# A hybrid encoder trunk on one core: unnormalised keys, with the squared norms put into the blocks' inversion, and six changes to the order of transfers and groups

## The chip, the core and the metric

The kernel runs on one core of a Trainium2 chip. The metric is the device time of one execution in microseconds, the median of three timed runs. A profile is of one further execution.

## The reference

The input is 1024 tokens of width 1024 in float32. Two layers follow, each a mixer and a SwiGLU feed-forward network (FFN, hidden width 2816) with RMS norms ahead of them, and a final norm. Layer 0 mixes with spatial gating and pooling, layer 1 with RWKV-7 time mixing, where the change lies:

```python
r = xr @ w_r; k = xk @ w_k; v = xv @ w_v
wlog = -jax.nn.softplus(-(w0 + jnp.tanh(xw @ w1) @ w2)) - 0.5
a = jax.nn.sigmoid(a0 + (xa @ a1) @ a2)
g = jax.nn.sigmoid(xg @ g1) @ g2
kk = heads(k * k_k)
kk = kk / jnp.maximum(jnp.sqrt(jnp.sum(kk * kk, axis=-1, keepdims=True)), 1e-12)
k = k * (1 + (a - 1) * k_a)
decay = heads(jnp.exp(-jnp.exp(wlog)))
# scan over the tokens, state S of 64x64 per head, inputs -kk and kk*a:
#   S = S*w + (S @ (-kk)) outer (kk*a) + v outer k ;  y = S @ r
y = wkv7_scan(rh, decay, kh, vh, -kk, kk * ah)
y = group_norm(y) * ln_w + ln_b
bonus = jnp.sum(rh * kh * r_k, axis=-1, keepdims=True) * vh
return ((y + bonus) * g) @ w_o
```

## The kernel before, in words

The tokens are two halves h of 512; a matrix product goes over blocks of 128 columns. Float32 products are made of three matmuls with operands split in a high and a low part (`mm3`, L399 to L401). Weights come in a fixed list (`plan`): ACT loads a block into `raw` (L121), ACT makes its high part (L157), DVE its low part (L158), and `take` hands the blocks out in list order. So the pushes in the list and the takes in the program must agree. Each engine runs its own instructions in a fixed order, which a scheduler has drawn from the program with priorities; the program can force an order of issue with `tc.issue_after`.

The stages that the change touches, in order of time:

- The FFN of layer 0 writes its hidden values to DRAM (`hid_d`). The down-projection of half 0 (`down_steps`, L883) goes over groups of two and three blocks (D0A): it loads the hidden blocks (`hd`, `ahi`, `alo`; L894), takes the weights and adds each sum to the residual H[0]. The residuals lie in DRAM too (`hm_d`); L1885 and L1891 load them. The same for half 1 (D0B[0]) runs beside the low-rank and gate products of half 0 (`beside`; LOWRANK_AT, GATE_AT and MIX_AT say after how many groups they come).
- `project(h)` makes, for eight pairs of heads p, the block of k, its square (for the norm), decays, r, and from them the scaled keys `ar` and `bk`. Ahead of that the gate's product is copied to `g_d` by ACT through buffers epx and k (L1212). For each pair, matmuls with a two-column indicator sum the squares (L1314) and the bonus (L1260). The norm is inverted on DVE and POOL (L1316, L404), sent to all rows by eight matmuls (L1333), and multiplied into the key (`kkn`, L1339). `interact` (L1238) multiplies keys and stores 32x32 blocks to `at_d`; after every fourth pair they are loaded as `iat` (L1253), and `invert` solves the triangular blocks in 31 steps of two DVE instructions (L1413, L1418), a few at a time between the other work. The inverses go to `xi_d` (L1422). Then the value product follows (L1384 on).
- `recur(h)` runs eight chunks of the recurrence, with FFN matmuls of the other half beside them. It loads `ar`, `bk`, `uv` and XT (the inverses, L1487 and L1490) for each chunk; the state is kept on chip between the halves in `state_d`.
- At the end FFN groups G1A[2] and G1A[3] of half 0, the output projection of half 1 between them, and the FFN of half 1. In `ffn` the kinds of step are g (gate), u (up), t (take a down weight) and d (down).

## Time and profile before

| | |
|---|---|
| three timed runs, median (lowest to highest) | 2438.87 us (2436.91 to 2441.32) |
| the profiled execution, its own time | 2432.77 us |
| its span in the trace | 2431.1 us |
| mean granted TensorE clock | 0.987 |
| bytes moved by DMA | 342.17 MB, 140 GB/s over the span |

In a row of a trace L399 is line 399 of the kernel; `out<-in` names what an instruction writes and reads; a time in brackets is the idle time of the engine before it and what ended that. PE is TensorE's matmul, PEld its weight load; DVE, ACT, POOL and SP are the vector, scalar, GpSimd and sync engines; a q behind a name is the engine's DMA-issuing side.

### The profile page before, as it was taken

To read this page: it belongs to the slowest core of one execution; us is meant where nothing else is said; L and a number is where in the kernel's file an instruction comes from. 1 tells how busy PE (TensorE), PEld (TensorE's weight loads), DVE (VectorE), ACT (ScalarE), POOL (GpSimd) and SP (SyncE) were. 2 spreads that over 40 slices of the span, in tenths; PEclk is the share of its full clock that TensorE was granted. 3 is DMA by queue.
4 is the path that set the end of the run, shared out by engine and by line. 5 is a ranking of instruction groups with operands and counts; after the bars stand their busy time and mean duration, and the time that the engine had idled before them with its cause. 6 is when DMAs were issued, how large, how long until landed. Compare 5 with 4: busy or idle time off the path is not lost. (4 is left out here: it accounts for less than half of the span.)

```text
span 2431.1 us, 38203 instructions
## 1 busy us (share of the span) xinstructions
PE 2347.3 (97%) x15567; PEld 1917.3 (79%) x15567; DVE 1475.1 (61%) x2328; ACT 937.1 (39%) x1403; POOL 214.8 (9%) x246
## 2 busy tenths in 40 slices
PE   8999999999899999999999999999999999999998
PEld 6888888888687878777777778777878788888887
DVE  6445765655567857856767947866664536444443
ACT  6233444444214753423335744433332224322223
POOL 0200000000000033201100123201100001000001
PEclk9999999999999999999999999999999999999999
DMA  5114443324665565775435465675544423433231
GB/s 179 52 52 147 152 152 96 121 96 165 226 233 172 171 163 133 207 202 167 143 117 168 150 169 142 190 232 159 146 121 132 123 77 97 144 98 96 86 105 52
DMA packets 406767, 342.17 MB, mean 141 GB/s; under 512 B 78080, under 2 KB 351616, under 8 KB 405824
## 3 DMA queue, kind: packets, MB, share of 16 engines
q10 hardware_dynamic: 266048, 195.33, 27.0%
q1 hardware_dynamic: 140544, 144.41, 19.1%
q8 instruction: 122, 2.00, 0.3%
q14 instruction: 53, 0.43, 0.1%
HBM read 263.07 MB, written 76.61 MB: 140 GB/s over the span
## 5 line engine op out<-in xcount | busy, mean ns | idle before, releaser
L399 PE MATMUL mm<-ahi,whi 128*128 128x512 f32 x1376 | 541.0, 394 | 7.0 <-ACT whi L157 3.0
L400 PE MATMUL mm<-alo,whi 128*128 128x512 f32 x1376 | 541.7, 394 | 2.6 <-DVE alo L158 2.5
L401 PE MATMUL mm<-ahi,wlo 128*128 128x512 f32 x1376 | 539.7, 392 | 1.6 <-DVE wlo L158 1.6
L157 ACT ACTIVATE whi<-raw 128x1024 fp32r<-128x1024 f32 (+1 forms) x280 | 282.1, 1014 | 572.2 <-PE mm L400 441.7
L158 DVE TENSOR_TENSOR wlo<-raw,whi 128x1024 fp32r<-128x1024 f32 (+1 forms) x280 | 328.5, 1177 | 249.8 <-ACT whi L157 231.5
L399 PEld LDWEIGHTS mm<-ahi,whi 128*128 128x128 f32 x1376 | 258.7, 188 | 66.2 <-ACT whi L157 4.7
L400 PEld LDWEIGHTS mm<-alo,whi 128*128 128x128 f32 x1376 | 258.8, 188 | 60.6 <-DVE alo L158 5.6
L401 PEld LDWEIGHTS mm<-ahi,wlo 128*128 128x128 f32 x1376 | 258.7, 188 | 57.9 <-DVE wlo L158 2.9
L493 DVE TENSOR_TENSOR h<-h,mm 128x512 f32<-128x512 f32 x276 | 185.8, 684 | 149.4 <-PE mm L401 148.4
L399 PE MATMUL mm<-hidhi,wdhi 128*128 128x512 f32 x304 | 118.4, 398 | 3.2 <-ACT hidhi L958 2.5
L400 PE MATMUL mm<-hidlo,wdhi 128*128 128x512 f32 x304 | 120.0, 395 | 0.0
L401 PE MATMUL mm<-hidhi,wdlo 128*128 128x512 f32 x304 | 119.7, 394 | 0.0
L730 PE MATMUL mm<-ahi,whi 128*128 128x512 f32 x296 | 115.6, 390 | 0.0
L731 PE MATMUL mm<-alo,whi 128*128 128x512 f32 x296 | 115.2, 389 | 0.0
L732 PE MATMUL mm<-ahi,wlo 128*128 128x512 f32 x296 | 113.6, 389 | 0.0
L955 DVE TENSOR_TENSOR sg<-sg,mm 128x512 f32<-128x512 f32 x52 | 35.7, 687 | 119.8 <-PE mm L401 119.6
L157 ACT ACTIVATE wdhi<-raw 128x1024 fp32r<-128x1024 f32 x42 | 43.3, 1056 | 160.2 <-PE mm L400 137.0
L399 PE MATMUL mm<-hd,dhi 128*128 128x512 f32 x192 | 75.9, 396 | 13.8 <-DMA hd<-hid_d 11.4
L400 PE MATMUL mm<-hd,dhi 128*128 128x512 f32 x192 | 75.8, 395 | 0.0
L401 PE MATMUL mm<-hd,dlo 128*128 128x512 f32 x192 | 74.9, 393 | 0.0
L399 PEld LDWEIGHTS mm<-hidhi,wdhi 128*128 128x128 f32 x304 | 57.7, 190 | 16.5 <-ACT hidhi L958 2.9
L400 PEld LDWEIGHTS mm<-hidlo,wdhi 128*128 128x128 f32 x304 | 57.9, 190 | 12.3 <-issue 0.5
(395 smaller groups left out, 4274.2 us busy)
## 6 DMA issues: line engine op xcount, KB each, us to landing
raw<-in_ffn_w_down_dram ACTq DMA_DIRECT2D x88, 512.0 KB
raw<-in_ffn_w_gate_dram ACTq DMA_DIRECT2D x74, 512.0 KB
raw<-in_ffn_w_up_dram ACTq DMA_DIRECT2D x74, 512.0 KB
hid_d<-hid SPq DMA_DIRECT2D x36, 512.0 KB
hd<-hid_d SPq DMA_DIRECT2D x26, 512.0 KB
raw<-in_ab_w_in_dram ACTq DMA_DIRECT2D x16, 512.0 KB
raw<-in_ab_w_out_dram ACTq DMA_DIRECT2D x16, 512.0 KB
raw<-in_rwkv_w_r_dram ACTq DMA_DIRECT2D x16, 512.0 KB
```

What stands on the lines that cost most here:

```text
L157: act.activation(hi, src, AF.Copy)
L158: (eng or dve).tensor_tensor(out=lo, in0=src, in1=hi.bitcast(F32), op=ALU.subtract)
L399: pe.matmul(o, whi, xhi, start=first, stop=False)
L400: pe.matmul(o, whi, xlo, start=False, stop=False)
L401: pe.matmul(o, wlo, xhi, start=False, stop=last)
L493: dve.tensor_tensor(out=H[h][:, m, :], in0=H[h][:, m, :], in1=o, op=ALU.add)
L730: pe.matmul(o, wh[:, k, :], x[0][:, k, :], start=st, stop=False, skip_group_check=True)
L731: pe.matmul(o, wh[:, k, :], x[1][:, k, :], start=False, stop=False, skip_group_check=True)
L732: pe.matmul(o, wl[:, k, :], x[0][:, k, :], start=False, stop=k == 3, skip_group_check=True)
L955: dve.tensor_tensor(out=s, in0=s, in1=o, op=ALU.mult)
```

## The change

The key is no longer divided by its norm. `kkn` is now k times k_k alone, on ACT. Where the block's factors are loaded for the inversion, the squared norms are loaded with them (`n2_d`, through DRAM): the block's factors are divided by the squared norms of their second index, and the inverse's diagonal starts with its reciprocal instead of with one. So the inverse holds the factor that the two key factors had, and the eight broadcast matmuls, the maximum on DVE and POOL's power are gone. The four norm matmuls and the four bonus matmuls follow one another; after every fourth pair `sums` copies the four pairs' sums, transposes them with one matmul and stores them.

Six other places: (1) the first hidden blocks of the down-projection are loaded ahead of the residual, whose second part (`rest_a`) follows in pieces; (2) the second half's down-projection has four hidden slots instead of three, loads a group ahead, and takes every third weight from the general ring; (3) the gate copies use eight buffers instead of four; (4) in `recur` the loads of norm weights, gate and values wait until the next key load has been issued, and the state passes through DRAM between the halves; (5) the last two groups of half 0 run in one call, with the output projection of half 1 and its norm called after the down step of the first; the gate step of the second group thereby comes ahead of that down step; (6) the low-rank product of the second half comes after six steps instead of eight.

```diff
-LOWRANK_AT, GATE_AT, MIX_AT = (2, 8), (3, 8), (1, 2)
+LOWRANK_AT, GATE_AT, MIX_AT = (2, 6), (3, 8), (1, 2)
...
-    push_ffn(1, 0, G1A[2], push_act(("y", 1), y_d[1]))
-    for e in push_o(1):
-        e()
-    push_ffn(1, 0, G1A[3])
+    y1, o1 = push_act(("y", 1), y_d[1]), push_o(1)
+    for i, e in enumerate(e for e in ffn_events(G1A[2] + G1A[3], True) if e[0] != "d"):
+        if e == ("u", G1A[3][0][0]):
+            for go in o1:
+                go()
+        push_ffn_event(1, 0, *e)
+        if e[0] in "gu":
+            next(y1, None)
...
-    def down_steps(h, groups, wslot, hslot, ahead=True, after=None, between=iter(()), at={}, first={}):
-
-        held = {}
+    def down_steps(h, groups, wslot, hslot, ahead=True, after=None, between=iter(()), at={}, first={}, loaded=None):
+
+        held, loaded = {}, [] if loaded is None else loaded
...
-                    sp.dma_start(held[f].bitcast(F32), hid_d[h][:, f])
+                    loaded.append(sp.dma_start(held[f].bitcast(F32), hid_d[h][:, f]).ins)
...
+                if ahead and gi + 1 < len(groups):
+                    load(groups[gi + 1])
                 if gi in at:
                     at[gi]()
-                if ahead and gi + 1 < len(groups):
-                    load(groups[gi + 1])
...
+                if f[-1] in then:
+                    then[f[-1]]()
...
-            t = tmp(("epx", "k")[m % 2], 2)
+            t = tmp(("k", "epx", "av", "sg")[m % 4], 2)
...
+                d2 = iat[:, 31, :]
                 for q in range(2):
                     sp.dma_start(
-                        iat[q * 64 : q * 64 + 64].rearrange("b s t -> b (s t)"),
-                        at_d[h][q, p - 3 : p + 1].rearrange("p r c s t -> (p r c) (s t)"),
+                        iat[q * 64 : q * 64 + 64, 0:31].rearrange("b s t -> b (s t)"),
+                        at_d[h][q, p - 3 : p + 1].rearrange("p r c s t -> (p r c) (s t)")[:, : 31 * 32],
                     )
+                    sp.dma_start(
+                        d2[q * 64 : q * 64 + 64], n2_d[h][q, p - 3 : p + 1].rearrange("p r c t -> (p r c) t")
+                    )
+                dve.tensor_scalar(out=d2, in0=d2, scalar1=1e-24, scalar2=None, op0=ALU.max)
+                dve.reciprocal(d2, d2)
+                dve.tensor_tensor(out=iat[:, 0:31], in0=iat[:, 0:31], in1=bc(d2.unsqueeze(1), [P, 31, 32]), op=ALU.mult)
...
+        def sums(p):
+
+            rn = tmp("rn", 1, [P, 64])[:, :32]
+            act.activation(rn, bo[:, 40 + 8 * p : 72 + 8 * p], AF.Copy)
+            ot = auxt()
+            pe.transpose(ot[:32, :P], rn, ident)
+            t = nt.tile([P, HT], F32, tag="nsq", bufs=2, name="n2")[:32, :P]
+            act.activation(t, ot[:32, :P], AF.Copy)
+            for q in range(2):
+                sp.dma_start(
+                    n2_d[h][q, p - 3 : p + 1].rearrange("p r (j c) t -> (p r j) c t", c=2),
+                    t.rearrange("m (c q t) -> m q c t", q=2, t=32)[:, q],
+                )
...
-            n2 = bo[:, 64 + 8 * p : 72 + 8 * p]
-            rn = tmp("rn", 2, [P, 4, 2, 8])[:, 0, 0, :]
-
-            def norms(j):
-                pe.matmul(n2[:, 2 * j : 2 * j + 2], sq[:, j * P : (j + 1) * P], ind2, start=True, stop=True)
-                if j == 3:
-                    dve.tensor_scalar(out=rn, in0=n2[:, 0:8], scalar1=1e-24, scalar2=None, op0=ALU.max)
-                    rsqrt(rn)
-
-            small = [lambda j=j: norms(j) for j in range(4)]
-            if prev is not None:
-                small += [lambda j=j, pv=prev: bonus(pv[0], pv[3], j) for j in range(4)]
+            n2 = bo[:, 64 + 8 * p : 72 + 8 * p].rearrange("t (r j) -> t r j", j=4)
+            o = o_r
             if p:
                 o = mmt()
-                dense2(o, *take(("r", h, p)), xr, between=small)
-            else:
-                o = o_r
-                for go in small:
-                    go()
+                dense2(o, *take(("r", h, p)), xr)
+            for j in range(4):
+                pe.matmul(n2[:, :, j], sq[:, j * P : (j + 1) * P], ind2, start=True, stop=True)
+            if prev is not None:
+                for j in range(4):
+                    bonus(prev[0], prev[3], j)
+            if p % 4 == 3:
+                sums(p)
             invert_on(INV)
-            rb = auxt()
-            for j in range(4):
-                for r in range(2):
-                    pe.matmul(
-                        rb[rows[r], j * P : (j + 1) * P], bc(rn[:, 2 * j + r : 2 * j + r + 1], [P, 64]), ident,
-                        start=True, stop=True,
-                    )
             ar, bk = tmp("ar", 2, [P, 8, 2, 64]), tmp("bk", 2, [P, 8, 2, 64])
             kkn = tmp("kkn", 2)
-            dve.scalar_tensor_tensor(out=kkn, in0=kt, scalar=col(C_KK + p), in1=rb, op0=ALU.mult, op1=ALU.mult)
+            act.activation(kkn, kt, AF.Copy, scale=col(C_KK + p))
...
-        pool.memset(xf[:, 0:2048:65], 1.0)
+        dve.tensor_copy(xf[:, 0:2048:65], iat[:, 31, :])
...
-    state_d = const.tile([P, 8, 64], F32, name="state_d")
-    pool.memset(state_d, 0.0)
+    state_d = dram.tile([P, 8, 64], F32, name="state_d")
...
-            sp.dma_start(bk, bk_d[h][c])
+            keys[0] = sp.dma_start(bk, bk_d[h][c])
...
+                if c == 7:
+                    sp.dma_start(state_d, Sn)
...
-                    with tc.issue_after(loaded[0].ins):
+                    with tc.issue_after(loaded[0].ins), tc.issue_after(keys[0].ins):
...
+        if h:
+            sp.dma_start(S[0], state_d)
...
-    wslot, hslot = slots_of(f, 4, 3)
+    wslot, hslot = slots_of(f, 4, 4)
     odd = {g: i % 2 for i, gs in enumerate(D0A) for g in gs}
-    prime_b, steps_b = down_steps(1, D0B[0], wslot, hslot, False, lambda m: sp.dma_start(h_d[1, 0][:, m, :], H[1][:, m, :]))
+    third = {g[2] for g in D0B[0]}
+    prime_b, steps_b = down_steps(1, D0B[0], lambda f: whl() if f in third else wslot(f), hslot, True, lambda m: sp.dma_start(h_d[1, 0][:, m, :], H[1][:, m, :]))
     acc, add = running_sums(0)
+    hid_loads = []
+
+    def rest_a():
+        for k in range(4, KT, 2):
+            with tc.issue_after(hid_loads[-1]):
+                sp.dma_start(H[0][:, k : k + 2, :], hm_d[0][:, k : k + 2, :])
+
     prime_a, steps_a = down_steps(
-        0, D0A, lambda f: (lw, wslot)[odd[f]](f), lambda f: (lh, hslot)[odd[f]](f), after=add, at={len(D0A) - 1: prime_b}, first=first,
+        0, D0A, lambda f: (lw, wslot)[odd[f]](f), lambda f: (lh, hslot)[odd[f]](f), after=add, at={0: rest_a, len(D0A) - 1: prime_b}, first=first, loaded=hid_loads,
...
-    for k in range(4, KT, 2):
-        a_loaded = sp.dma_start(H[0][:, k : k + 2, :], hm_d[0][:, k : k + 2, :])
...
-            with tc.issue_after(a_loaded.ins):
+            with tc.issue_after(hid_loads[-1]):
                 sp.dma_start(H[1][:, k : k + 2, :], hm_d[1][:, k : k + 2, :])
...
-    drive(ffn(1, 0, hnA, f, G1A[2], between=take_act(("y", 1)), early=True))
-    exhaust(out_proj(1, ys))
-    hnB = norm_split(1, C_FFN + 8, b)
-    drive(ffn(1, 0, hnA, f, G1A[3], last=True, early=True))
+    hnB = []
+
+    def out_b():
+        exhaust(out_proj(1, ys))
+        hnB.extend(norm_split(1, C_FFN + 8, b))
+
+    drive(ffn(1, 0, hnA, f, G1A[2] + G1A[3], last=True, between=take_act(("y", 1)), early=True, then={G1A[2][0][-1]: out_b}))
```

SyncE's issues at the start of the down-projection, before (`hm_d_75` and `hm_d_76` hold the residuals of halves 0 and 1, `hid_d_77` half 0's hidden values):

```order
L743 DMA hid_d_78<-hid 128x1024
L1885 DMA h<-hm_d_75 128x1024 x2
L1891 DMA h<-hm_d_76 128x1024 x4
L894 DMA hd<-hid_d_77 128x1024 x3
L894 DMA ahi<-hid_d_77 128x1024
L894 DMA alo<-hid_d_77 128x1024
L894 DMA hd<-hid_d_77 128x1024 x3
```

The first three hidden blocks stand behind six residual loads. The same place now (L898 is the hidden load, L1903 and L1916 the residual's):

```order
L747 DMA hid_d_78<-hid 128x1024
L898 DMA hd<-hid_d_77 128x1024 x3
L1903 DMA h<-hm_d_75 128x1024 x2
L898 DMA hd<-hid_d_77 128x1024
L898 DMA ahi<-hid_d_77 128x1024
L898 DMA alo<-hid_d_77 128x1024
L1916 DMA h<-hm_d_76 128x1024 x2
L898 DMA hd<-hid_d_77 128x1024 x2
L1916 DMA h<-hm_d_76 128x1024 x2
L898 DMA hd<-hid_d_77 128x1024
```

The first three hidden blocks now stand ahead of all six residual blocks, which are now spread between the later hidden loads.

TensorE's matmuls in a middle pair of `project(0)`, before (`aux<-ident,rn` is the broadcast of the norm, `aux<-ar,bk` the interaction, `bo<-ind,k` the bonus):

```order
L401 MATMUL mm<-xhi,wlo 128x512
L1238 MATMUL aux<-ar,bk 64x64 x16
L1333 MATMUL aux<-ident,rn 64x128 x8
L1291 MATMUL aux<-tw,w_6325 128x512
L1292 MATMUL aux<-twlo,w_6325 128x512
L1291 MATMUL aux<-ta,a_6326 128x512
L1292 MATMUL aux<-talo,a_6326 128x512
L1260 MATMUL bo<-ind_6460,k 128x2 x4
L399 MATMUL mm<-ahi,whi 128x512
```

Broadcast and bonus stand on either side of the four decay matmuls. The same place now, where `aux<-ar,bk` again is the interaction:

```order
L405 MATMUL mm<-xhi,wlo 128x512
L1319 MATMUL aux<-tw,w_6326 128x512
L1320 MATMUL aux<-twlo,w_6326 128x512
L1319 MATMUL aux<-ta,a_6327 128x512
L1320 MATMUL aux<-talo,a_6327 128x512
L1245 MATMUL aux<-ar,bk 64x64 x16
L403 MATMUL mm<-ahi,whi 128x512
```

The broadcast is gone from here, the bonus too, and the interaction has moved behind the decays. And TensorE between that pair's key product and the next r product (`bo<-ind,kkn` are the norms):

```order
L404 MATMUL mm<-alo,whi 128x512
L405 MATMUL mm<-ahi,wlo 128x512
L1344 MATMUL bo<-ind_6461,kkn 128x2 x4
L1274 MATMUL bo<-ind_6461,k 128x2 x4
L403 MATMUL mm<-xhi,whi 128x512
L404 MATMUL mm<-xlo,whi 128x512
```

The bonus has moved to behind the norms, in one run with them.

VectorE at the start of the first inversion, now (`iat` holds the factors and, in its last row, the squared norms; L1427 and L1432 are the steps' two instructions):

```order
L1268 TENSOR_SCALAR iat<-iat 128x32
L1269 RECIPROCAL iat<-iat 128x32
L1331 SCALAR_TENSOR_TENSOR cum<-smask,sg 128x256 x2
L1422 COPY xi<-iat 128x32
L1354 SCALAR_TENSOR_TENSOR ar<-kkn,epx 128x8x63
L1369 TENSOR_TENSOR ar<-mm,epx 128x8x64
L158 TENSOR_TENSOR wlo<-raw,whi 128x1024
L1270 TENSOR_TENSOR iat<-iat 128x992
L1365 TENSOR_TENSOR bk<-kkn,em 128x8x64
L1363 TENSOR_TENSOR k<-k,av 128x512
L1427 TENSOR_TENSOR it<-iat,xi 128x31
L1364 TENSOR_TENSOR bk<-k,em 128x8x64
L1432 TENSOR_TENSOR xi<-xi,it 128x31
```

Maximum, reciprocal, the diagonal's copy and the multiplication of 992 columns now stand ahead of the first step, with key and weight instructions between them.

More of the change, by code (lines that the diff above doesn't have):

```diff
@@ L930, in slots_of, with ffn @@
         )
-    def ffn(l, h, hn, fp, groups=GROUPS, last=False, nd=3, after=None, between=iter(()), early=False):
+    def ffn(l, h, hn, fp, groups=GROUPS, last=False, nd=3, after=None, between=iter(()), early=False, then={}):
         dests["d"] = lambda: (fp.tile([P, D], F32R, tag="wdhi", bufs=nd, name="wdhi"),
@@ L1045, in tile_trunk @@
     xi_d = [dram.tile([2, 8, 2, 8, 32, 2, 32], F32, name=f"xi_d{h}") for h in range(2)]
+    n2_d = [dram.tile([2, 8, 2, 8, 32], F32, name=f"n2_d{h}") for h in range(2)]
     at_d = [dram.tile([2, 8, 2, 8, 32, 32], F32, name=f"at_d{h}") for h in range(2)]
@@ L1361, in project @@
             bonus(prev[0], prev[3], j)
-        bs = tmp("rn", 2, [P, 4, 2, 8])
+        bs = tmp("rn", 1, [P, 64]).rearrange("t (j r p) -> t j r p", j=4, r=2)
         dve.tensor_copy(bs, bo[:, 0:64].rearrange("t (j p r) -> t j r p", p=8, r=2))
@@ L1452, in recur @@
         lnw = wt("lnw", 1, [P, 8, 64])
-        C, ypair, loaded = {}, [], [None]
-        S, Q, last = [state_d], {}, []
+        C, ypair, loaded, keys = {}, [], [None], [None]
+        S, Q, last = [wt("S", 2, [P, 8, 64])], {}, []
+        if h == 0:
+            pool.memset(S[0], 0.0)
         def ordered(f, *args, **kw):
@@ L1588, in burst @@
             if cg < NCH - 1:
-                Sn = state_d if c == 7 else wt("S", 2, [P, 8, 64])
+                Sn = wt("S", 2, [P, 8, 64])
                 os_ = smt()
```

## The prediction

> **What bounds the kernel now.** I read the page's busy shares first, then PE's waits, then a table of stretches around the longest of them.
>
> ```profile
> PE 2347.3 (97%) x15567; PEld 1917.3 (79%) x15567; DVE 1475.1 (61%) x2328; ACT 937.1 (39%) x1403; POOL 214.8 (9%) x246
> ```
>
> TensorE is busy for 2347.3 of 2431.1 us, so the time is its list of matmuls plus its gaps. Only two things help: fewer matmuls, or shorter gaps with what follows them. The gaps by releaser (line, what it waited for, us in total, times, longest):
>
> ```profile
> PE mm L399 <- DMA hd<-hid_d: 11.4, 2, 9.8
> PE sm L1460 <- DMA bk<-bk_d: 8.8, 4, 6.0
> ...
> PE mm L399 <- ACT ahi L157: 3.8, 3, 1.9
> ...
> PE aux L1238 <- DVE bk L1351: 3.3, 2, 2.3
> ...
> PE mm L399 <- ACT epx L1212: 2.8, 2, 1.5
> ```
>
> One gap is long, the down-projection's start (hd); the others are of one or two microseconds, most of them in the two projections. The next table has, for chosen stretches, the length, the busy time of PE, PEld, DVE, ACT and POOL, then the granted clock, DMA share and GB/s.
>
> ```profile
> 625.00:630.00 5.00, 1.94 (x9) 1.28 (x7) 4.98 (x7) 0.00 (x0) 0.00 (x0) 1.00 1.01 366
> 630.00:635.00 5.00, 0.00 (x0) 0.00 (x0) 0.00 (x0) 0.00 (x0) 0.00 (x0) 0.55 1.03 419
> 635.00:640.00 5.00, 3.31 (x8) 2.67 (x9) 1.94 (x2) 2.11 (x2) 0.00 (x0) 0.50 1.03 409
> 940.00:960.00 20.00, 18.23 (x107) 14.52 (x106) 17.30 (x37) 5.80 (x9) 5.58 (x6) 0.74 0.49 130
> 960.00:980.00 20.00, 20.00 (x137) 16.93 (x135) 18.76 (x35) 13.01 (x21) 9.04 (x7) 1.00 0.44 113
> 980.00:1000.00 20.00, 17.96 (x135) 13.82 (x134) 19.87 (x34) 9.64 (x14) 6.90 (x6) 0.83 0.65 187
> 1270.00:1290.00 20.00, 14.81 (x51) 9.58 (x50) 12.06 (x16) 9.08 (x12) 0.20 (x1) 0.91 0.84 248
> 1395.00:1415.00 20.00, 14.73 (x56) 10.93 (x55) 6.32 (x6) 9.81 (x14) 2.61 (x7) 0.91 0.83 227
> 1495.00:1515.00 20.00, 18.40 (x136) 14.90 (x137) 19.27 (x39) 6.68 (x10) 6.55 (x6) 0.91 0.53 142
> 1515.00:1535.00 20.00, 20.00 (x154) 16.81 (x149) 18.78 (x36) 13.84 (x22) 8.84 (x7) 1.00 0.44 115
> 1535.00:1555.00 20.00, 14.91 (x105) 11.38 (x104) 18.00 (x38) 8.40 (x12) 8.25 (x3) 1.00 0.62 163
> 1930.00:1940.00 10.00, 7.37 (x25) 5.25 (x23) 6.18 (x8) 4.13 (x5) 0.00 (x0) 0.83 0.58 172
> ```
>
> A gap costs its idle time and, in most of these stretches, a spell at half clock: 940 to 960 loses 20 - 18.23 = 1.8 us of idle time and (1 - 0.74) x 20 = 5.2 us of clock. Wherever DVE nears 20 of 20 (940 to 1000, 1495 to 1555), it is as close to being the bound as PE: there the first inversion of each half runs beside the projection.
>
> **The change part by part.** All sums are against the profiled execution (2432.77 us, span 2431.1, so 1.7 us lie outside the span); it is 6.1 us below the median of the three timed runs, 2438.87. I take the differences off that median.
>
> *A. Start of the first down-projection.* SyncE's issues there, and PE's first matmul behind them:
>
> ```profile
> 621.62 0.79 SPq L1885 DMA_DIRECT2D h<-hm_d  x2
> 622.51 1.89 SPq L1891 DMA_DIRECT2D h<-hm_d  x4
> 624.45 2.75 SPq L894 DMA_DIRECT2D hd<-hid_d  x3
> ```
> ```profile
> 636.69 0.76 PE L399 MATMUL mm<-hd,dhi 128*128 128x512 f32 x1 [9.75 <-DMA hd<-hid_d]
> ...
> 640.94 0.39 PE L400 MATMUL mm<-hd,dhi 128*128 128x512 f32 x1
> 641.17 0.40 PE L401 MATMUL mm<-hd,dlo 128*128 128x512 f32 x1
> ```
>
> Nine transfers of 512 KB stand in one line with the DMA engines saturated (share 1.01 to 1.03, about 410 GB/s, so 1.3 us each). The three hd that PE needs come last: 9 x 1.3 us from 621.6 ends at 633, and PE begins at 636.7. The loss is 9.75 us idle and half of the 3.31 busy us up to 640 (1.65): 11.4. With hd first, 3 x 1.3 from 621.6 ends at 625.5; before it was 3.5 us from that arithmetic to the first matmul, so 629 at the latest, against 626.8 when PE has run out: 0 to 2.2 us stay. Behind that the two h (2.6 us more) hold the sums of m = 4 to 7 and so four of the five PSUM banks; one group of nine matmuls (at full clock one starts every 0.23 us, 640.94 to 641.17: 2 us) covers most. I take -10, bounds -6 (hd waits for its memory until 624.45 as now) and -11.4. The later h transfers move behind, where DMA has room once the start is over.
>
> *B. Second half's down-projection.* One hd slot more and loads ahead take the other hd wait (11.4 - 9.8 = 1.6) and some of the ahi waits (3.8 in three, one of them at 1274 outside this stage). I take -3, bounds 0 and -4.5: the weight splits of ACT and DVE can be what is late next.
>
> *C. Norms without the broadcast.* The broadcast of 1/norm, one run in a pair and the matmul after it (eight matmuls, each in two pieces):
>
> ```profile
> 875.26 1.09 PE L1333 MATMUL aux<-ident,rn 128*64 128x128 f32 x16
> 876.29 0.50 PE L1291 MATMUL aux<-tw,w 128*128 128x512 f32 x1
> ```
> A run takes 876.29 - 875.26 = 1.03 us, and about 0.1 us of changing over on either side: 1.17 us a pair, for eight pairs in each half. Five pairs of each half lie outside the DVE-heavy stretch: 5.85 us, less two transposes of the sums at 0.35 each (an eighth of a 1.03 us run is 0.13; a lone fp32 one has no cover, hence more): -5.1 a half. Norm and bonus matmuls are as many as before; in one run instead of two saves at most 0.1 us a pair, and I count nothing. POOL's pow goes, and with it the wait for rn; POOL is busy 9%.
>
> In the DVE-heavy stretch PE alone would gain its three broadcasts (3.5), its idle time and its clock: 3.5 + 1.8 + 2.0 + 8.6 = 15.9 in half 0, 3.5 + 1.6 + 5.1 + 1.8 = 12 in half 1. DVE caps that. Its rows for the inversion's steps and the multiplication kkn that moves to ACT:
>
> ```profile
> L1418 DVE TENSOR_TENSOR xi<-xi,it 128x31 f32<-128x31 f32 (+15 forms) x124 | 45.8, 370 | 2.3
> L1413 DVE TENSOR_TENSOR it<-iat,xi 128x31 f32<-128x31 f32 (+15 forms) x124 | 45.3, 365 | 13.9 <-POOL xi L1408 6.0 <-DMA iat<-at_d 5.1
> ...
> L1339 DVE SCALAR_TENSOR_TENSOR kkn<-k,vec,aux 128x512 f32<-128x512 f32 x16 | 11.9, 742 | 24.9 <-PE aux L1333 24.9
> ```
>
> Each pair takes from DVE 0.74 us and a small maximum (below the 0.37 us of the inversion's steps; I take 0.2); each block adds a multiplication of 992 columns (0.74 x 992 / 512 = 1.4, an estimate), and about 0.6 for maximum, reciprocal and copy. DVE's work in 940 to 1000 is 17.30 + 18.76 + 19.87 = 55.9, becoming 55.9 - 2.8 + 2.0 = 55.1; in 1495 to 1555 it is 56.05, becoming 55.3. DVE's bound leaves 4.9 and 4.7 us of 60 to gain. I take these, nearest to the rows of DVE; bounds 0 (the same stretches as now) and the PE figures (15.9, 12).
>
> *D. Gate copies.* One copy of the gate, on ACT, and its wait for the store that empties its buffer:
>
> ```profile
> 854.48 0.60 ACT L1212 ACTIVATE epx<-mm 128x512 f32<-128x512 f32 x1 [1.85 <-DMA g_d<-epx]
> ```
>
> Eight buffers instead of four take epx's 2.8 us and k's part; 1395 to 1415 lost 5.3 idle and 1.8 clock, of which 2.5 waits on a load that stays. -1.8 in half 0, -4.5 in half 1; bounds 0 and -7. The multiplication kkn that DVE loses is on ACT one such copy, 0.6 us a pair; ACT is idle for 6 us or more of each 20 in the table, so it costs nothing there, and up to 0.6 us a pair if ACT were late.
>
> Sum for the projections: half 0 -5.1 - 4.9 - 1.8 = -11.8; half 1 -5.1 - 4.7 - 4.5 = -14.3.
>
> *E. The squared norms' way through DRAM* adds two stores and two loads a block on SyncE. They stand ahead of the inversion, whose slack is at its end:
>
> ```profile
> 1049.04 1.12 SPq L1422 DMA_DIRECT2D xi_d<-xi  x2
> ...
> 1056.56 0.54 SPq L1487 DMA_DIRECT2D XT<-xi_d  x1
> ```
>
> The inverse is stored at 1049.04 and read at 1056.56: 7.5 us of cover, against 2 to 4 us of way (two issues each way of 0.5 to 1.1 us by these rows). I count 0; with the cover gone it is up to 4 us a half. The Trainium skill ("DMA: Bandwidth & Descriptors", section "Why small descriptors are slow (HBM only)") speaks against such rows of 128 bytes: small pieces move far below the line rate. No row here shows the price of these, and the sum would change only by what exceeds the cover.
>
> *F. Recurrence.* Norm weights, gate and values now wait until the keys' load is issued; two of PE's four bk waits lie behind them:
>
> ```profile
> 1102.47 1.10 PE L1460 MATMUL sm<-ar,bk 64*64 64x128 f32 x32 [1.12 <-DMA bk<-bk_d]
> ```
>
> The second half has the same wait (8.8 - 6.0 leaves 2.8 for the three short ones). What waits instead are those norm weights, gate and values, which only the end of a chunk needs, and whatever SyncE issues behind them. -2, bounds 0 and -2.8. The state's way through DRAM is one 256 KB store and load with a whole stage between; 0, at worst 1 us.
>
> *G. Last groups in one run.* The next gate product stands between the up product and the down-projection that waited for its split:
>
> ```profile
> 1934.74 1.65 PE L399 MATMUL mm<-hidhi,wdhi 128*128 128x512 f32 x3 [2.51 <-ACT hidhi L958]
> ```
>
> 24 matmuls at 0.23 us, 5.5 us, now cover 2.5 us. The stretch 1930 to 1940 lost 2.63 + 1.7 = 4.3; I take -4, bounds -2 (the half clock stays and a new norm chain of half 1 runs late) and -4.3.
>
> *H. Low-rank step earlier* (after six, not eight, steps in half 1): normalisation and mixing start earlier, but the second norm's broadcast stands directly ahead of the FFN that needs it. In 1270 to 1290 5.2 us idle and 1.8 clock wait for splits of y that stay. 0, bounds -4 and +4.
>
> Total: -10 - 3 - 11.8 - 14.3 - 2 - 4 = -45.1; 2438.87 - 45.1 = 2393.8, rounded to 2394.
>
> **The rivals.**
> 1. *DVE bounds more than I allow.* The static order puts reciprocal and multiplication ahead of a pair's keys; PE waits for them and the stretches at 940 and 1495 stay as they are. For it: 19.87 of 20 us busy. The 9.6 us of the caps go, and some broadcasts outside too (about 4): 2394 + 14 = 2408.
> 2. *The half clock stays.* It follows some gaps (940 to 960: 1.8 us idle, 0.74) and not others (1535 to 1555: 5.1 us idle, 1.00). If it comes from short low-work matmuls, which stay, and not from the gaps, the clock's part of D, G and A, 1.8 + 1.7 + 1.65, and the part within the caps (about 5) stay: 2394 + 10 = 2404. The Trainium skill ("TensorE: Matmul & The Clock Gate", Part 1) would have it so: it halves the clock only after an idle window of about 3.4 us. The row at 940, with 1.8 us in two pieces, differs, so I give this one little.
> 3. *Slower: the second inversion falls behind the value loop.* If its factors come so late that it begins as the loop ends, its 31 steps of 0.735 us, 22.8 us, stand bare ahead of the recurrence in each half, with about 2 us of half clock behind: 2 x 24.8 = 49.6 more, 2443.5 to 2446 with the other bounds against. It decides from a lateness of 7.5 + 22.5 = 30 us a half. Against it: the way through DRAM is a few us, and the sums precede the last interaction in PE's list.
> 4. *The change doesn't do what it says at the down-projection.* hd's memory isn't free earlier than 624.45, or the two h that hold the banks come late: A brings 4 and not 10, B nothing: 2403.
>
> **How the numbers follow.** Forecast 0.58, rival 1 0.17, rival 2 0.08, rival 3 0.04, rival 4 0.09, several of these at once 0.04 (to 2432). About 0.2% of the time, 4.9 us, is what a measurement can tell from no change. The forecast's own range is the sum with the projection caps at 0 (2404) and with half of the PE figures instead of the caps (2394 - 9 - 3 = 2382), less a little for G and H: 2380 to 2406. The range takes in rivals 1, 2 and 4 with their own spread: 2379 to 2418. Faster by over 0.2% are all but rival 3 and part of the last: 0.93; same 0.03; slower 0.04.
>
> **What would show it.** The row of hd's first matmul should have a wait under 3 us and the clock stay at 1.00 there. L1333's group must be gone and two 32-column transposes a half be there; the wait for rn too. In the DVE-heavy stretches DVE should be at 19 or more of 20 and PE's gaps name DVE. The wait on hidhi at the end should be gone. I am wrong if PE waits on XT or iat's followers for over 5 us, if the projections take as long as now, or if the new order opens waits above 10 us in sum at the low-rank step, the recurrence or the last groups.

## The result and the profile after

The changed kernel takes 2413.31 us (median of four runs, 2410.52 to 2414.85), the kernel before 2438.18 us beside it; the ratio is 0.9913, 95% interval 0.9897 to 0.9928. The two medians differ by 25 us where 45 were forecast; the ratio stands for 21 us, its interval for 18 to 25. The profiled execution took 2410.52 us, its span is 2408.8 us against 2431.1, which is 22 us less.

The page's first part of the changed kernel:

```profile
PE 2327.8 (97%) x15315; PEld 1904.6 (79%) x15315; DVE 1467.8 (61%) x2312; ACT 947.7 (39%) x1427; POOL 180.4 (7%) x226
```

PE has 252 records fewer (the broadcasts, less the transposes) and is busy 19.5 us less. Its idle time over the whole span hardly changed: 81.0 us against 83.8, and the mean granted clock is 0.987 in both. So nearly all that was gained in the end is work that left PE; the gaps and the half clock that went at some places came up at others. The gaps of PE by releaser, the longest five groups:

```profile
PE sm L1475 <- DVE gt L1522: 12.6, 5, 6.7
PE aux L1245 <- DVE bk L1365: 6.6, 5, 2.0
PE aux L550 <- DMA vrow<-in_mix_norm_dram: 6.4, 1, 6.4
PE mm L403 <- ACT whi L157: 6.2, 4, 4.1
PE sm L1477 <- DMA bk<-bk_d: 5.5, 2, 3.3
```

hd, epx and rn have gone from the list. At its head stands gt, a step of the recurrence, which had 2.9 us in all before; the wait for whi has doubled.

To see where the time went I cut both traces at the same matmuls: the first of the gate product of each half (ghi, whi), the last of the value product, the last of the second half's first-layer down-projection (hd, wlo), the first on hidhi of the group before the last two (1934.74 before, 1906.34 after), and the last of all. The cuts around the first recurrence, of before and then of after:

```profile
1035.69 0.39 PE L1387 MATMUL mm<-whi,xlo 128*128 128x512 f32 x1
...
1272.98 0.39 PE L401 MATMUL mm<-hd,wlo 128*128 128x512 f32 x1
```
```profile
1004.93 0.39 PE L1401 MATMUL mm<-whi,xlo 128*128 128x512 f32 x1
...
1245.73 0.39 PE L405 MATMUL mm<-hd,wlo 128*128 128x512 f32 x1
```

| stage (us) | before | after | difference | forecast |
|---|---|---|---|---|
| start to gate 0 (A, B) | 847.7 | 833.3 | -14.4 | -13 |
| projection 0 (C, D) | 188.0 | 171.7 | -16.4 | -11.8 |
| recurrence 0 and down-projection | 237.3 | 240.8 | +3.5 | -1 |
| output projection 0, low rank, first FFN group (H) | 122.6 | 126.3 | +3.7 | 0 |
| projection 1 (C, D) | 190.8 | 178.8 | -12.1 | -14.3 |
| recurrence 1, up to the last groups (F) | 348.4 | 355.6 | +7.2 | -1 |
| last groups to the end (G) | 487.9 | 494.3 | +6.4 | -4 |

The last two rows together are called the last stage: 836.3 us before, 849.8 after, +13.6. The start and the two projections bring what was forecast and a little more: together -42.9 against -39.1. The other four stages lose 20.8 us where 6 were to be gained.

A stage is read from one execution of each kernel, and one execution scatters. Eight kernels (the whole change and e3, e4, e7, e8, e12, e13 and e14 below) have the same instructions in the same order on ACT, DVE, POOL and PE from the start to the end of recurrence 0. Their projection 0 took 171.7 to 178.3 us, and their recurrence 0 took 238.8 to 243.0. So a difference of a few us in one stage of one execution shows nothing by itself. Recurrence 0 did get longer: the lists of before took 237.3 us, and 235.5 in a second execution (e9, whose lists are the same there but for two small copies).

The places of A and of the stretches that DVE fills, in the changed kernel. First SyncE's issues and PE's first matmul on hd:

```profile
619.95 1.75 SPq L898 DMA_DIRECT2D hd<-hid_d  x3
622.56 1.01 SPq L1903 DMA_DIRECT2D h<-hm_d  x2
```
```profile
627.62 0.39 PE L403 MATMUL mm<-hd,dhi 128*128 128x512 f32 x1
```

No wait stands before it: hd was issued even before the 621.6 us that I had reckoned from. Some stretches of both inversions, with busy times of PE, PEld, DVE, ACT and POOL, clock, DMA share and GB/s:

```profile
905.00:925.00 20.00, 20.00 (x132) 16.95 (x131) 16.85 (x35) 8.99 (x14) 3.77 (x6) 1.00 0.58 143
925.00:945.00 20.00, 19.86 (x122) 16.14 (x120) 19.29 (x35) 9.89 (x15) 5.27 (x7) 1.00 0.50 135
945.00:965.00 20.00, 17.51 (x109) 13.85 (x109) 18.73 (x34) 13.39 (x22) 8.67 (x5) 1.00 0.47 125
1470.00:1490.00 20.00, 20.00 (x127) 16.74 (x126) 18.95 (x38) 9.66 (x15) 4.97 (x8) 1.00 0.49 123
1490.00:1510.00 20.00, 18.62 (x117) 15.05 (x115) 19.49 (x34) 14.72 (x24) 7.08 (x5) 1.00 0.45 119
```

DVE is at 18.7 to 19.5 of 20 us in all but the first, PE is idle 2.6 us in the first sixty, and the clock stays at 1.00. Just behind them, in 965 to 970, it is 0.66. Over all of projection 0 it is 0.99, against 0.95 before.

Now the losses. The first is at the start of each recurrence. Rows of SyncE and then PE's first matmul of recurrence 0, before and after:

```profile
1049.04 1.12 SPq L1422 DMA_DIRECT2D xi_d<-xi  x2
1052.11 2.15 SPq L1477 DMA_DIRECT2D bk<-bk_d  x1
...
1062.08 0.32 PE L1462 MATMUL sm<-ar,bk 64*64 64x128 f32 x1
```
```profile
1024.37 1.13 SPq L1436 DMA_DIRECT2D xi_d<-xi  x2
1027.56 2.03 SPq L1492 DMA_DIRECT2D bk<-bk_d  x1
...
1037.40 0.29 PE L1477 MATMUL sm<-ar,bk 64*64 64x128 f32 x1 [2.16 <-DMA bk<-bk_d]
```

SyncE issues the first keys' loads (ar, then bk) right behind the store of the second inverse, and PE's first step needs those keys. Counted from the end of the value product (1035.69 and 1004.93), the store comes at 13.4 us before and 19.4 after, PE's first step at 26.4 and 32.5. In half 1 the store comes at 19.9 and 24.9, the first step at 32.6 and 38.2. The projection got shorter, the inversion less so. Of the 16.4 and 12.1 us that the projections gained, 10.2 and 6.4 reach the first step. It is so in all eleven kernels with unnormalised keys (first step at 30.6 to 34.8 us in half 0, 35.9 to 41.3 in half 1) and in none of the five with normalised keys (26.4 to 27.0, 32.6 to 34.3). What it costs was not tested: PE has other matmuls meanwhile, and its idle time just before the first step is 2.2 and 3.3 us, against 0 and 2.1 before.

The longest new gap is in the last chunk of recurrence 1, PE first, then ACT, then DVE:

```profile
1744.54 1.77 PE L1475 MATMUL sm<-ar,bk 64*64 64x128 f32 x27 [6.74 <-DVE gt L1522]
```
```profile
1733.54 0.35 ACTq L121 DMA_DIRECT2D raw<-in_ffn_w_down_dram  x1
1739.73 1.06 ACT L157 ACTIVATE wdhi<-raw 128x1024 fp32r<-128x1024 f32 x1 [6.91 <-DMA raw<-in_ffn_w_down_dram]
```
```profile
1734.59 0.68 DVE L959 TENSOR_TENSOR sg<-sg,mm 128x512 f32<-128x512 f32 x1
1740.82 1.93 DVE L158 TENSOR_TENSOR wdlo<-raw,wdhi 128x1024 fp32r<-128x1024 f32 x1 [5.54 <-ACT wdhi L157]
1742.67 1.21 DVE L158 TENSOR_TENSOR wlo<-raw,whi 128x1024 fp32r<-128x1024 f32 x1
1743.81 1.28 DVE L1522 TENSOR_TENSOR gt<-sm,gm 128x512 f32<-128x512 f32 x2
```

DVE's list holds gt behind two weight splits; the first waits for a high part, and that for a load issued at 1733.54 and usable at 1739.73. So a recurrence step that has nothing to do with this weight waits for its transfer, and PE with it. The gap is no chance of one execution: e3 and e7 have the same order on DVE at this place, and wait 7.3 and 6.6 us there.

At the last groups, two rows of PE and ACT's issues ahead of the second:

```profile
1906.34 0.96 PE L403 MATMUL mm<-hidhi,wdhi 128*128 128x512 f32 x3 [2.96 <-ACT hidhi L962]
...
2045.92 0.79 PE L403 MATMUL mm<-ahi,whi 128*128 128x512 f32 x1 [4.05 <-ACT whi L157]
```
```profile
2038.83 0.40 ACTq L121 DMA_DIRECT2D raw<-in_ffn_w_gate_dram  x1
...
2044.81 1.06 ACT L157 ACTIVATE whi<-raw 128x1024 fp32r<-128x1024 f32 x1 [2.33 <-DMA raw<-in_ffn_w_gate_dram]
```

The wait for hidhi, which G was to take, is still there. It belongs to the down step of the group before the merged ones: 24 matmuls on hidden values with wdhi and wdlo stand there (eight times three), which is one hidden block, the group [17], and not [18, 19]. The second row is new: the load of the next FFN's first gate weight is issued at 2038.83, behind ACT's work for the final norm of half 0, and PE runs dry at 2041.9.

At H, the second norm's broadcast (L451) now stands directly ahead of the products that need it:

```profile
1325.20 1.10 PE L451 MATMUL aux<-ndg,ones 128*128 128x512 f32 x2
...
1327.84 0.98 PE L403 MATMUL mm<-ahi,whi 128*128 128x512 f32 x3 [1.55 <-ACT ahi L157]
...
1330.79 0.50 PE L404 MATMUL mm<-alo,whi 128*128 128x512 f32 x1 [1.98 <-DVE alo L158]
```

### The profile page after: what moved, and what is told of

It reads as the page before. It is cut to its first block, busy times and chain, and to the rows that moved or that the text cites. A ratio compares the mean times of both kernels' runs of the same rounds, so it can differ in the third digit from the quotient of the medians.

```text
span 2408.8 us, 37648 instructions
## 1 busy us (share of the span) xinstructions
PE 2327.8 (97%) x15315; PEld 1904.6 (79%) x15315; DVE 1467.8 (61%) x2312; ACT 947.7 (39%) x1427; POOL 180.4 (7%) x226
## 4 chain that ended last, share of the span: by engine, by line
PE 78%; DVE 8%; DMA 6%; issue 2%; ACT 2%; POOL 2%; SPq 1%; ACTq 0%; POOLq 0%; DVEq 0%
PE mm L403 17%; PE mm L404 17%; PE mm L405 17%; PE mm L734 5%; PE mm L736 5%; PE mm L735 5%; PE sm L1475 4%; DVE wlo L158 1%; DVE h L497 1%; PE yp L1475 1%; PE aux L1399 1%; PE mm L584 1%; PE mm L585 1%; PE aux L1400 1%; PE aux L1401 1%
## 5 line engine op out<-in xcount | busy, mean ns | idle before, releaser
L157 ACT ACTIVATE whi<-raw 128x1024 fp32r<-128x1024 f32 (+2 forms) x284 | 286.2, 1014 | 509.9 <-PE mm L404 385.8
L158 DVE TENSOR_TENSOR wlo<-raw,whi 128x1024 fp32r<-128x1024 f32 (+2 forms) x284 | 337.0, 1191 | 232.0 <-ACT whi L157 208.2
L403 PEld LDWEIGHTS mm<-ahi,whi 128*128 128x128 f32 x1376 | 259.8, 189 | 70.5 <-ACT whi L157 8.2
L157 ACT ACTIVATE wdhi<-raw 128x1024 fp32r<-128x1024 f32 x42 | 43.3, 1057 | 162.2 <-PE mm L404 124.6
L158 DVE TENSOR_TENSOR wdlo<-raw,wdhi 128x1024 fp32r<-128x1024 f32 x42 | 53.2, 1266 | 30.5 <-ACT wdhi L157 30.3
L405 PEld LDWEIGHTS mm<-hidhi,wdlo 128*128 128x128 f32 x304 | 57.4, 189 | 12.2 <-issue 0.3
L734 PEld LDWEIGHTS mm<-ahi,whi 128*128 128x128 f32 x296 | 55.6, 188 | 11.7 <-issue 0.2
```

Of the source, the lines that this page charges most:

```text
L157: act.activation(hi, src, AF.Copy)
L158: (eng or dve).tensor_tensor(out=lo, in0=src, in1=hi.bitcast(F32), op=ALU.subtract)
L403: pe.matmul(o, whi, xhi, start=first, stop=False)
L405: pe.matmul(o, wlo, xhi, start=False, stop=last)
L734: pe.matmul(o, wh[:, k, :], x[0][:, k, :], start=st, stop=False, skip_group_check=True)
```

## The experiments

Two theories stood at first. Theory 1: each loss belongs to one of the six places. Theory 2: the recurrences have a pace of their own and give back what is gained ahead of them. All ratios are to the kernel before, with 95% intervals; stages are cut as above, and are of one execution each, while the times are medians of 4 to 10 runs.

**e1: the unnormalised keys alone.** The kernel before with the hunks on n2, `sums`, `kkn`, iat and the diagonal.

> The kernel before with the unnormalised keys alone (no change of order at the six places). Theory 1, each loss belongs to one of the six places: the two projections gain nearly what they gained in the whole change without the gate copies (about 22 us of 28.5) and the recurrences stay at 225 and 232 us, so about 2416 us. Theory 2, the recurrences have a pace of their own (steps on DVE and loads in a fixed order) and give back what the projections gain: the projections gain 22, the recurrences are 10 to 15 us longer, about 2428 us.

Measured 2429.82 us, ratio 0.9978 (0.9967 to 0.9989). The projections fall from 188.0 to 174.6 and from 190.8 to 178.8, 25.4 us in all. Recurrence 0 takes 242.6 (+5.3), the last stage 845.1 (+8.8), and the stage of the output projection 131.6 us (+9.0), which nothing in this kernel touches. Theory 2 has the right size, but not the place: the third stage is no recurrence.

**e2: the six places alone**, keys normalised as before.

> The six changes of order alone, keys normalised as before. Theory 1: down-projections -14.4, gate copies about -5, against +4 at the low-rank step, +4 to 6 at the last groups and about +15 in the recurrences: about 2438 + 4 = 2442 us. Theory 2: the projections hardly shrink, so the recurrences keep their 225 and 232 us: 2438 - 19 + 9 = about 2428 us.

Measured 2430.07 us, 0.9979 (0.9968 to 0.9990). The time is theory 2's, the reason isn't: projection 1 shrinks by only 3.2 us and the last stage is still 12.1 us longer, recurrence 0 with its down-projection 6.2.

So each part alone brings about 5 us by its ratio, both together 21, though the gains at their own places are 25 and 20 us. Both parts and the whole lose about the same, 18 to 23 us, in stages behind. This gave theory 3: the lists of the engines behind any edit are drawn anew by the scheduler, and the lists of before were a favourable draw.

**e3: last groups in two calls again.** The hunk on `y1, o1` and the one on `out_b` undone.

> The whole change without place 5 (the last two groups in two calls again, the output projection between them). Both theories: the wait of 4.2 us for whi after the last down step falls to the 0.6 + 0.7 us of before, so 3 to 4 us less, about 2409.5 us. Had the merging taken the wait for hidhi, as forecast, it would be 4 us more, 2417: the wait of 3.1 us there should be as long in both.

Measured 2407.61 us, 0.9891 (0.9873 to 0.9909); its interval overlaps the whole change's. The last groups to the end take 488.4 us instead of 494.3; recurrence 1 ahead of them, whose lists are the same, took 358.0 against 355.6, so that the last stage is only 3.4 us shorter (846.4). No wait for whi is left at the end, and the row of the group before is as it was in the kernel before:

```profile
1906.93 1.65 PE L399 MATMUL mm<-hidhi,wdhi 128*128 128x512 f32 x3 [2.57 <-ACT hidhi L958]
```

The merging costs about 6 us and takes no wait. The other kernels agree: all five with merged groups wait 3.6 to 4.1 us for whi and take 493.0 to 494.6 us from the last groups to the end; the ten others, e12 apart, have no such wait and take 487.1 to 488.9.

**e4: low rank after eight steps.**

```diff
-LOWRANK_AT, GATE_AT, MIX_AT = (2, 6), (3, 8), (1, 2)
+LOWRANK_AT, GATE_AT, MIX_AT = (2, 8), (3, 8), (1, 2)
```

> The whole change with the low-rank step after eight steps again. Theory 1: the stage of output projection and first FFN group falls from 126.3 to about 122.6 us, nothing else changes, about 2409.5 us. Theory 2: the same there, but the recurrence of half 1, whose fixed order is drawn anew behind it, may move by 5 us either way: 2404 to 2415.

Measured 2408.29 us, 0.9891 (0.9874 to 0.9908). The stage is 123.0 us, 3.3 less, and the two waits behind L451 are gone. With six steps it took 124.6 to 127.8 us (the whole change, e3, e7, e13), with eight 121.6 to 123.8 (e4, e8, e12, e14), so that the 3 us are clear of scatter. Projection 1 is 3.7 us shorter too, against 4.7 more in projection 0, where the lists are the same: that is scatter.

**e5: the gate copies alone**, one line in the kernel before.

```diff
-            t = tmp(("epx", "k")[m % 2], 2)
+            t = tmp(("k", "epx", "av", "sg")[m % 4], 2)
```

> The kernel before with eight buffers for the gate copies and nothing else. Theory 1, each loss belongs to its place in the change: the waits for epx and k go, 1.5 to 3 us a half, the recurrences stay at 225 and 232 us, about 5 us faster than before. Theory 3, any change ahead of a recurrence draws its fixed order anew and the order of before is a favourable draw: the same gain ahead of it, but recurrence and following stages 5 to 15 us longer in sum, with waits at other places than before; between 2 us faster and 10 us slower than before.

Measured 2437.81 us, 1.0013 (1.0002 to 1.0025): slower. Projection 0 gains 4.3 us, projection 1 0.8, the output projection's stage 3.2; recurrence 0 is 7.9 longer and the last stage 7.4. The profiled execution was the slowest of the ten, 4 us over their median, so a part of this is scatter. Theory 1 fails here all the same: by its ratio the kernel is not 5 us faster, as that theory has it.

**e6: the first hidden blocks alone**, A without B.

> The kernel before with the first hidden blocks ahead of the residual and nothing else (three hidden slots as before). Theory 1: 10 to 11 us less at the down-projection, all else the same: about 2425 us. Theory 3: the same 10 to 11 us there, given back by 5 to 20 us in stages that the edit doesn't touch: 2430 to 2440 us.

Measured 2432.43 us, 0.9992 (0.9982 to 1.0001). The start to gate 0 is 11.3 us shorter, as it should be, and recurrence 0 is 12.9 longer. The gain is there and is given back 200 us later; ten timed runs say the same, with about 2 us of it left.

**e7: the whole change without the wait for the keys.**

```diff
-                    with tc.issue_after(loaded[0].ins), tc.issue_after(keys[0].ins):
+                    with tc.issue_after(loaded[0].ins):
```

> The whole change, but norm weights, gate and values don't wait for the next key load. Theory 1, with this wait as what lengthened the recurrences: they return to 225 and 232 us, about 2403 us, and the two waits of 1.1 us on bk are back. Theory 3: the waits on bk are back, the recurrences are neither as before nor as in the whole change: 2405 to 2425 us.

Measured 2420.09 us, 0.9935 (0.9915 to 0.9956). ACT, DVE and POOL run the whole change's lists here; only SyncE's order differs. The two waits for keys are back as expected, and longer than in the kernel before: 2.65 us at 1082.1 and 2.73 at 1638.8. The last stage is 856.2, 6.4 longer than in the whole change; the intervals of the two times overlap. The wait for the keys did not lengthen the recurrences, and it takes the two waits that it was made for.

**e8: last groups and low rank both as before**, e3 and e4 together.

> The whole change with the last groups in two calls and the low-rank step after eight steps, both as before. If the two costs add (5.7 and 5.0 us by their own runs), about 2402 us. Theory 3: the end's part (4 us) is kept, since nothing is drawn anew behind it; the low-rank step's part is partly chance: 2402 to 2412 us.

Measured 2396.10 us, 0.9849 (0.9830 to 0.9868): 17 us faster than the whole change and the fastest of all. That is 6 us more than the 10.7 of e3 and e4 together, which these few runs don't set apart from chance. Its last stage takes 838.7 us, 11.1 less than in the whole change: 6.6 of these are the last groups', 4.6 recurrence 1's (351.0). e4 runs the same lists as e8 through recurrence 1 and took 357.4 there, so the 4.6 are within scatter. Recurrence 0 takes 241.8. What has changed for sure is DVE's list at the place of the long gap, here in e8:

```profile
1735.03 0.68 DVE L955 TENSOR_TENSOR sg<-sg,mm 128x512 f32<-128x512 f32 x1
1735.63 1.22 DVE L158 TENSOR_TENSOR wlo<-raw,whi 128x1024 fp32r<-128x1024 f32 x1
1736.77 0.68 DVE L959 TENSOR_TENSOR hidlo<-sg,hidhi 128x512 fp32r<-128x512 f32 x1
1737.37 1.28 DVE L1518 TENSOR_TENSOR gt<-sm,gm 128x512 f32<-128x512 f32 x2
```

One split stands between sg and gt instead of two, and its load is there. PE waits 1.5 us for gt here, and 3.2 in e4, which has the same order; with two splits ahead of gt it waited 6.6 to 7.3.

**e9: nothing but two small copies, in the kernel before.** A constant is copied onto itself at the head of each projection.

```diff
         pool.memset(ind2[64:128, 1:2], 1.0)
+        [dve.tensor_copy(smask, smask) for _ in range(2)]
```

> The kernel before with two copies of a 128x256 constant onto itself on DVE at the head of each projection (under 0.4 us each, no other work and no other data). They change 372 rows of PE's list, all in the last third of the second recurrence. Theory 1: at most 1 us, within 0.1% of before. Theory 3, the list that is drawn anew is worse than the tuned one: second recurrence to output projection 2 to 10 us longer than 443 us, all ahead of it the same; 1 to 10 us slower.

Measured 2440.19 us, 1.0022 (1.0004 to 1.0039). The last stage is 839.4 us, 3.1 longer, which is within scatter; the timed runs are 0.2% slower, just clear of no change, as theory 3's lower end has it.

**e10 and e11: the same on e8**, two DVE copies, or three ACT copies instead.

> The kernel of e8 with the same two DVE copies. They change 2428 rows of PE's list, from the first recurrence on. Theory 1: at most 1 us, 2396 to 2398 us. Theory 3: the two recurrences with what follows move by several us, up or down: 2388 to 2412 us, with waits at other places than in e8.

> The kernel of e8 with three ACT copies of the same constant onto itself in place of the DVE ones; 2043 rows of PE's list change, from the first recurrence on. Theory 1: at most 1 us. Theory 3: another draw, 2388 to 2412 us, differing from e10 by several us.

e10 measured 2402.03 us, 0.9871 (0.9843 to 0.9898); the interval overlaps that of e8. Its last stage is 849.4 us against 838.7. e11 measured 2412.20 us, 0.9907 (0.9891 to 0.9924): 16 us slower than e8 (14 by the ratios), clear of it, for six copies of a small constant. Recurrence 0 takes 247.2 (+5.4), the output projection's stage 129.8 (+6.0), the last stage 846.8 (+8.1). And the long gap is back, with the same rows of DVE ahead of it as in the whole change:

```profile
1755.92 1.34 PE L1471 MATMUL sm<-ar,bk 64*64 64x128 f32 x20 [7.70 <-DVE gt L1518]
```
```profile
1751.35 2.78 DVE L158 TENSOR_TENSOR wdlo<-raw,wdhi 128x1024 fp32r<-128x1024 f32 x1 [5.65 <-ACT wdhi L157]
1754.05 1.21 DVE L158 TENSOR_TENSOR wlo<-raw,whi 128x1024 fp32r<-128x1024 f32 x1
1755.19 1.27 DVE L1518 TENSOR_TENSOR gt<-sm,gm 128x512 f32<-128x512 f32 x2
```

e8 and e11 compute the same with the same transfers. What differs, the copies apart, is the order of the lists, and with it where the splits stand in DVE's.

**e12: another pace for recurrence 1 on e8**, RATIO 2.0 instead of 3.0.

> The kernel of e8 with the pace constant of the second recurrence (RATIO) at 2.0 instead of 3.0, so that the recurrence's steps are taken later beside the FFN; rows change from the middle of the second recurrence on. Theory 3: the stages up to there as in e8, second recurrence to output projection between 440 and 456 us where e8 has 446: 2390 to 2406 us. Theory 1: no loss there to be had, since before had 443: 2394 to 2398 us.

Measured 2447.83 us, 1.0063 (1.0037 to 1.0090), outside what both theories expected. The last stage is 891.9 us: the recurrence's last matmul comes 358 us behind the value product instead of 240 in e8, and a part of it (1850 to 1870) runs at a clock of 0.51. It says nothing on the theories, only that the pace must not go this way.

**e13 and e14: the low parts of the down weights on POOL** beside recurrence 1, in the whole change and in e8.

```diff
+    splits["d"] = lambda n, src, hi, lo: split(src, hi, lo, pool)
     drive(ffn(1, 0, hnA, f, G1A[1], early=True), recur(1, wp, in_pieces(hp, 0, h_d[0, 1])), RATIO)
+    splits.pop("d")
```

> The whole change with the low parts of the down weights that run beside the second recurrence split on POOL instead of DVE (POOL is idle there). Theory 3 with its mechanism, a step of the recurrence queued on DVE behind a weight split whose load is late: the wait of 6.9 us on gt goes or falls under 2 us, since that split no longer stands ahead of gt; second recurrence to output projection from 455 to about 448 us, about 2405 us, if the rest of the new draw is neutral. If the wait on gt is the recurrence's own chain, it stays as long as it is, and the time too.

> The kernel of e8 (last groups and low-rank step as before) with the same splits on POOL. e8 has no such wait (its longest on gt is 1.7 us), so by the mechanism there is 1 to 3 us to be had: 2392 to 2398 us; a new draw may add up to 10 us. If POOL at more than twice DVE's time per split becomes the late one, PE waits on wdlo from POOL, and it is slower than e8 by that.

e13 measured 2419.16 us, 0.9938 (0.9922 to 0.9955); e14 2407.30, 0.9886 (0.9868 to 0.9904). The gap on gt is gone from that place in e13. PE's waits of these three kinds in the whole kernel are now:

```profile
PE sm L1475 <- DVE gt L1522: 4.4, 3, 3.3
PE sm L1475 <- ACT uv L1597: 3.7, 3, 2.8
PE sm L1475 <- DVE Q L1575: 3.7, 2, 2.6
```

The cause of that gap is so confirmed: it goes with the splits, from 12.6 us on gt in all to 4.4. The time isn't: at the same place PE now waits 2.6 us for Q and 2.8 for uv, the wait for the first keys of recurrence 1 is 7.7 us (5.5 to 6.1 in e4, e7, e8, e10 and e11), and the last stage is 856.3. e14 loses 5.5 us in its last stage against e8, and 5.3 in projection 1, where its lists are still e8's: so scatter alone makes as much.

## Why the prediction was wrong, point by point

The direction was right, the measured time lies in the range, and the size was about twice too large. What was forecast for the start and the projections came. The step that failed is the other part of the sum: everything behind the projections was held fixed or put down as a gain (E 0, F -2, G -4, H 0, in all -6), and the runs show +20.8 us there: +3.5 and +7.2 in the two recurrences, +3.7 at H, +6.4 at G.

**A and B held**: -14.4 against -13. hd first in SyncE's order takes the whole wait and the half clock behind it. Rival 4 is out.

**C and D held**, -28.5 against -26.1 with the caps. e1 and e5 split them: the norms 25.4, the copies 5.1 by themselves. These are single executions; the eight with the same lists put projection 0 at 171.7 to 178.3 us, against 188.0 and 188.3 with the lists of before, so the gain is sure and its size is known to some 3 us. Rival 1 is out in the projections: DVE is at 18.7 to 19.5 of 20 us in most of the stretches, as the cap had it, but PE loses little there. It came back behind them, at E. What I had not counted is that DVE also stands idle, 14.7 us in all, for the squared norms' loads (four waits for iat<-n_d); no PE wait is put down to it.

**Rival 2 did not come at these places**: the half clock at hd is gone, and projection 0 has a mean clock of 0.98 to 0.99 in the eight executions, against 0.95 before. The clock differs between executions of the same lists, too: projection 1 had 0.98 in the kernel before and 0.96 in e9. Over the whole kernel nothing was won; the mean clock is 0.987 in both, with new half-clock spells at new gaps (0.53 in 1744 to 1748, 0.71 in 2041 to 2050). Why the gaps at 940 were followed by half clock stays open. The Trainium skill ("TensorE: Matmul & The Clock Gate", Part 1) puts the half clock after an idle window of about 3.4 us; a gap of 6.7 us in the changed kernel is followed by that 0.53, which agrees, and the 1.8 us at 940 in the kernel before don't.

**Rival 3 is out in its size, but E failed by its mechanism.** The second inversion begins ahead of the value product's end, and nothing in the recurrence waits on XT for more than 2.4 us at once. But E's "7.5 us of cover" was no slack: between 1049.04 and 1056.56 SyncE issues the loads of keys and values, and these stand behind the inverse's store. The store now comes 6 us later behind the value product in half 0 and 5 in half 1, and with it the recurrence's first step. How much of the +3.5 and +7.2 us is due to this is open, since recurrence 0 is longer in e2, e5 and e6 too (243.5 to 250.2 us), whose first step is not late.

**F held at its place and failed as a sum.** The two waits of 1.1 us, one in each half, are gone with the keys' wait and back without it (e7). What failed is that all else in the recurrences was held fixed. It isn't fixed: an edit can change the lists behind it. Recurrence 0 with its down-projection, 237.3 us before, takes 235.5 to 250.2 in the other fifteen kernels, above 237.3 in all but one (e9, whose lists are those of before). Recurrence 1 up to the last groups takes 351.0 to 362.4, e12 apart, against 348.4. The sum had no term for this.

**G failed, the step "24 matmuls at 0.23 us, 5.5 us, now cover 2.5 us".** The row 1934.74 belongs to the group before the merged ones. The count of matmuls behind the row (24, one block) would have told it. The merging took no wait, and put 4.05 us of PE's wait and a spell of half clock at the end: 6 us more instead of 4 less. The likely reason is that 24 matmuls fewer stand between the output projection and the next FFN, while ACT's final-norm work holds up its own weight loads; this was read from the rows, not tested by itself.

**H failed by its size**: 0 with bounds -4 and +4, measured +3.7 in its stage and 3.3 when undone. The uncovered broadcast is what the step named; nothing came against it.

**The range's lower end** doesn't follow from its words. Half of the PE figures (15.9 and 12) is 14 us, 4 more than the caps' 9.6, so by these words it would be 2390 and not 2382; the 3 us of that line come from no row.

**What stays open.** That lists which do the same work differ by some 14 to 16 us is shown by e8 and e11, and one of the mechanisms by their rows and by e13. Of the 20.8 us lost in the whole change, about 6 are G's and 3 H's. The rest, some 11 us in the two recurrences, is not divided between the later inversion and the new lists; no run moves the keys' loads ahead of the inverse's store. Only G, H and the keys' wait were undone in the changed kernel, so the other places are not cleared. That the lists of before were a favourable draw, and that its constants were chosen with them on a chip, was not tested.

## What to carry to other kernels

Where a scheduler draws fixed lists for in-order engines, an edit can change the lists far behind it: compare by stage and not only by total, test an edit of no work (a copy of a constant onto itself), and take a second execution of the same lists to learn how far a stage scatters. A gain that is real at its place (11 us in e6) can be lost behind it, and two parts that bring 5 us each alone can bring 21 together, so parts shouldn't be rejected by their totals. When a stage gets shorter, look for what it covered: here the inversion and the loads queued behind its store. A step of a chain that has little work waits as long as whatever stands ahead of it on its engine: a split of a late-loading weight is better behind it. Taking the splits away took the wait (e13), though not the time.

## What was not expected of the hardware

Six copies of a 128x256 constant on ACT move the time by 16 us (2396.10 to 2412.20) through the order of the lists. Spells of half clock differ between executions of the same lists: projection 1 had a mean clock of 0.98 in the kernel before and 0.96 in e9, with the same lists on all engines but for two copies. POOL needs 2.42 us for a low part of 128x1024 where DVE needs 1.2; sixteen of them, 38.7 us of its time, ran beside the recurrence in e13, which was no faster for it.
